# A hybrid decoder layer with a 16-expert MoE: weights loaded in groups of 128 rows, the routing of the last tile reordered, and gaps that move fp32r operands

## Chip, cores and metric

One core of a Trainium2 chip runs the whole kernel. The metric is the device time of one execution in microseconds (us). TensorE (PE) multiplies, with its weight loads shown apart as PEld; VectorE (DVE), ScalarE (ACT) and GpSimd (POOL) do the rest, and SyncE (SP) issues the weight transfers.

## What is computed

One decoder layer in fp32 on 512 tokens of width 1024: four token mixers with a gated merge, then a mixture of experts (top 1 of 4 groups, top 2 of its 4 experts), then a final RMSNorm.

```python
h = h + hybrid_mixer(rms_norm(h, norm1_g), ...)   # n @ w_in, 4 mixers, gates * (y_b @ P_b), merged @ w_out
h = h + hier_moe(rms_norm(h, norm2_g), ...)       # 16 experts, D = 1024, F = 512
return rms_norm(h, final_norm_g)

# hier_moe
in_grp = exp_logits of the best group;  top_l, top_e = lax.top_k(in_grp, 2)
hid = silu(t @ w_gate[e]) * (t @ w_up[e]) * combine[:, e]
out = sum over e of hid @ w_down[e]
```

## The kernel before

**Products.** An fp32 product is made of three fp32r matmuls: `split` (L118) cuts an operand into a high part (ACT, a copy to fp32r) and a low part (DVE, the difference), and `mm3` (L122) runs three: both high parts (L123), the streamed ("moving") operand's low part with the loaded ("stationary") operand's high part (L124), and the reverse (L125). In the groups of the trace `b<-nl,XH` names the moving operand first.

**Stages.** From the start of the span: norm and transposes to 27 us; the W_in projections with the attention between them to 286 us; gates and branch products (`b<-nh,hi` and `b<-yh,hi`) to 548 us; the output product `wo_mm` (`b<-nh,m`, `b<-woh,m`) with the routing of tiles 0 to 2 to 597 us; the routing of the last tile and the dispatch to 616 us; the experts to about 925 us; the weighted sum for the last two experts, the final norm and the stores.

**Order of the work.** PE's order is the order of the code (manual_schedule, L1043). On DVE, ACT, POOL and SP a scheduler fixes the order; each runs its list in order, and an instruction that waits holds all that stand behind it.

**Weights of the experts.** Each of the 16 experts has G (gate), U (up) and D (down), 2 MB each. `wload` (L1012) brings 1 MB at a time into a ring of 13 buffers of 1 MB, SP issuing a load as soon as a buffer is free; partition p takes rows 8p to 8p+7 of G and U (4p to 4p+3 of D), so half a weight is one 8 KB run in each partition. `gsplit` (L1215) splits 128x1024 pieces into four slots `nh`, `nl`, two ahead of their use. So the k-th row group of a product is every 8th (G, U) or 4th (D) row, and everything multiplied with it is read with a stride of 32 or 16 bytes: `h2` in `disp` (L1156), X in `xt` (L1228), H in `h_tr` (L1243) and `h_half` (L1318).

**Expert loop** (L1424 on). For expert e: half of G (L123 `b<-nh,XH`), the transposes of H of e-1 (L1247), the other half of G, the transposes of X of e+1 (L1234), D of e-1 (`x<-nh,HH`), U of e. Experts 0 and 15 have no neighbour to fill waits, so their U goes through `up_halves` (L1326): two column halves of 256, with the moving operand read in a pattern of pairs, so that the first half of H can be transposed while the second is multiplied.

**Routing.** `r_t` (L1058) transposes a tile of x, `r_mm` (L1068) makes the logits and then, on DVE, the norm's scale and the top-2 choice up to the selection matrix `Msel`; `r_h2` (L1100) makes the normed tile h2; `r_pos` (L1106) counts positions on PE (L1111, L1112), makes the one-hot `sel` of expert 0 (L1116) and then positions, scatter (POOL, L1131) and weights; `disp` (L1156) multiplies h2 by `sel` into the input of expert 0 (L1160), 8 products a tile. After the last `wo_mm` the order is r_t(3,0), half of disp(0), r_t(3,1), the other half, r_mm(3), r_pos(2), r_h2(3), disp(1), disp(2), r_pos(3), disp(3), then the counts (L1202). `ph` (L1294) are 8 one-hots made on POOL for the weights `ws`, which PE needs (L1385) between G and U of expert 0. `pT` (L1407) are 8 one-hots for the last two experts, made on POOL beside expert 14, ahead of the gather of all experts' rows (L1372).

Of the kernel before, what the change touches and what calls it, by code (L numbers as in the profile page):

```python
# [85 lines left out]
def hybrid_layer_kernel(ctx, tc, x, norm1_g, w_in, gm_norm_g, gm_ws, gm_b, conv_w, conv_b, lru_wa,  # L86
# [982 lines left out]
    def r_mm(t):  # L1069
        p = bank()  # L1070
        for k in range(KD):
            PE.matmul(p[:, :24], xTb[t % 2][:, k], wr[:, k], start=k == 0, stop=k == KD - 1)
        s2 = sm("s2", 1)
        V.tensor_tensor(s2, ss2[:, t, 0:1], ss2[:, t, 1:2], op=OP.add)
        r2 = rs2[:, t:t + 1]
        rstd(r2, s2, D)
# [20 lines left out]
        V.tensor_tensor(Msel[t], OH[:, 0], OH[:, 1], op=OP.add)  # L1097
        XS[t] = OH, ef, lg, g8, e8

    def r_h2(t):  # L1100
        h2 = h2b[t]
        V.scalar_tensor_tensor(h2, x1[:, t], rs2[:, t:t + 1], g2b, op0=OP.mult, op1=OP.mult)
        XS[t] += (h2,)

    scat = []

    def r_pos(t):
        OH, ef, lg, g8, e8, h2 = XS[t]
        p = bank()
        for tt in range(t):  # L1110
            PE.matmul(p[:, :16], ones, Msel[tt], start=tt == 0, stop=False)  # L1111
        PE.matmul(p[:, :16], upper, Msel[t], start=t == 0, stop=True)  # L1112
# [3 lines left out]
        V.tensor_scalar(sel, slot, p[:, 0:1], o0, op0=OP.is_equal, op1=OP.mult)  # L1116
# [35 lines left out]
        XS[t] = sel, h2  # L1152

    x0 = [bank("x0", 2), bank("x0", 2)]

    def disp(t, ks=range(KD)):  # L1156
        sel, h2 = XS[t]
        hv = h2.rearrange("p (q k) -> p k q", k=KD)
        for k in ks:
            PE.matmul(x0[k // 4][:, (k % 4) * 128:(k % 4 + 1) * 128], hv[:, k], sel, start=t == 0 and k % 4 == 0, stop=t == NT - 1,  # L1160
                      skip_group_check=True)

    def run(g, n=99):
# [11 lines left out]
    for t in range(NT):  # L1175
        g = wo_mm(t, 1)
        for i in range(KD):
            next(g)
            if pend:
                pend.pop(0)()  # L1180
        run(g)
        wb.append([mgp.tile([128, 2048], FT, name=f"m{t}")])
        load(len(wb))
        while pend:
            pend.pop(0)()
        no = lambda: None
        pend = [lambda t=t: r_t(t, 0), no, lambda t=t: r_t(t, 1), no, lambda t=t: (r_mm(t), r_h2(t)), no, no,
                ] + ([lambda t=t: r_pos(t - 1)] if t else [])
# [12 lines left out]
    for t in range(NT):  # L1201
        PE.matmul(pcnt[:, :16], ones, Msel[t], start=t == 0, stop=t == NT - 1)  # L1202
# [23 lines left out]
        return s  # L1226

    def xt(X, q):  # L1228
        Xv = X.rearrange("p (q k) -> p k q", k=KD)
        ps_ = []  # L1230
        for i in range(2):
            p = bank()
            for k in range(4):
                PE.transpose(p[:, k * 128:(k + 1) * 128], Xv[:, i * 4 + k], ident)  # L1234
# [7 lines left out]

    def h_tr(H):  # L1243
        p = bank()
        Hv = H.rearrange("p (q k) -> p k q", k=4)
        for k in range(4):
            PE.transpose(p[:, k * 128:(k + 1) * 128], Hv[:, k], ident)  # L1247
# [13 lines left out]
    Yt = hl_pair(hl)  # L1261
    Xt = hl_pair(hl) + hl_pair(hl2)
    Yt.append(Xt.pop())
    for X in Xt[1:]:
        G.memset(X, 0.0)
    regs = {}

    def x_load(e):
        regs[e] = G.value_load(cnt[0:1, e:e + 1], min_val=0, max_val=T)
        X = Xt[(e - 1) % 3]  # L1270
        if e == 1:
            G.dma_start(X, XE[e * CAP:e * CAP + CAP])
            return X
        for r in range(4):
# [27 lines left out]
    def run_up(k, e, js):  # L1302
# [4 lines left out]
        if js[-1] == 3 and k == "U":  # L1307
            V.tensor_tensor(H[e], H[e], pgu[k], op=OP.mult)
        elif js[-1] == 3:
            H[e] = Ht[e % 2]  # L1310
            if e in (0, NE - 1):
                o, i = [v.rearrange(a, s=2, q=128) for v, a in ((H[e], "p (s q c) -> p q s c"),
                                                                (pgu[k], "p (q s c) -> p q s c"))]
                A.activation(o, i, AF.Silu)
            else:
                A.activation(H[e], pgu[k], AF.Silu)
# [59 lines left out]
    for e in range(NE):  # L1376
# [173 lines left out]
```

## Time and profile before

| what | us |
|---|---|
| median of 3 runs | 951.55 (951.45 to 951.55) |
| the profiled execution | 951.25 |
| its span on the chip | 949.7 |
| PE busy | 922.9 |
| DVE busy | 627.8 |
| ACT busy | 538.8 |
| POOL busy | 101.2 |

The busy time of PE is a sum over overlapping matmuls: the duration of one is longer than the step from its start to the next start. A row of the timeline gives start, duration, engine, line, operation, out<-in, shape, and in brackets the idle time ahead of it and what ended it. A row of the groups gives the count, the sum of durations and the mean in ns. A row of the windows gives the busy time of PE, PEld, DVE, ACT and POOL in a stretch, then the granted PE clock as a share of full speed, the share of the DMA engines' time and GB/s.

### The profile page before, as it was taken

To read this page: it belongs to the slowest core of one execution; us is meant where nothing else is said; L and a number is where in the kernel's file an instruction comes from. 1 tells how busy PE (TensorE), PEld (TensorE's weight loads), DVE (VectorE), ACT (ScalarE), POOL (GpSimd) and SP (SyncE) were. 2 spreads that over 40 slices of the span, in tenths; PEclk is the share of its full clock that TensorE was granted. 3 is DMA by queue.
4 is the path that set the end of the run, shared out by engine and by line. 5 is a ranking of instruction groups with operands and counts; after the bars stand their busy time and mean duration, and the time that the engine had idled before them with its cause. 6 is when DMAs were issued, how large, how long until landed. Compare 5 with 4: busy or idle time off the path is not lost. (4 is left out here: it accounts for less than half of the span.)

```text
span 949.7 us, 13038 instructions
## 1 busy us (share of the span) xinstructions
PE 922.9 (97%) x4765; PEld 760.1 (80%) x4765; DVE 627.8 (66%) x1165; ACT 538.8 (57%) x837; POOL 101.2 (11%) x181
## 2 busy tenths in 40 slices
PE   8999999999999999999999999999999999999993
PEld 7979888777768888888888888977888888888882
DVE  6677457888773343444374515658989989999955
ACT  7436548558982232232263314247888888888853
POOL 2000000000000000000000011441110101110750
PEclk9999999999999999999999999999999999999997
DMA  8558456652124224222444437679999999999283
GB/s 246 143 147 283 164 192 222 218 182 89 45 74 129 65 90 131 89 89 89 133 132 163 172 117 288 253 231 332 357 355 397 377 369 382 393 386 380 66 163 110
DMA packets 90047, 195.73 MB, mean 206 GB/s; under 512 B 7388, under 2 KB 63784, under 8 KB 78712
## 3 DMA queue, kind: packets, MB, share of 16 engines
q1 hardware_dynamic: 62312, 153.56, 46.2%
q0 software_dynamic: 6528, 20.29, 7.6%
q10 hardware_dynamic: 21136, 20.98, 6.4%
q8 instruction: 39, 0.64, 0.3%
q14 instruction: 32, 0.26, 0.1%
HBM read 166.24 MB, written 34.60 MB: 211 GB/s over the span
## 5 line engine op out<-in xcount | busy, mean ns | idle before, releaser
L120 DVE TENSOR_TENSOR lo<-raw,hi 128x1024 fp32r<-128x1024 f32 (+3 forms) x70 | 79.0, 1132 | 129.4 <-ACT hi L119 129.1
L119 ACT ACTIVATE hi<-raw 128x1024 fp32r<-128x1024 f32 (+3 forms) x70 | 68.6, 986 | 161.0 <-PE b L124 88.0
L123 PE MATMUL b<-nh,XH 128*128 128x512 f32 (+1 forms) x272 | 109.9, 404 | 0.5 <-ACT XH L119 0.5
L125 PE MATMUL b<-nh,XL 128*128 128x512 f32 (+1 forms) x272 | 108.2, 398 | 0.0
L124 PE MATMUL b<-nl,XH 128*128 128x512 f32 (+1 forms) x272 | 108.1, 397 | 0.0
L123 PE MATMUL b<-nh,hi 128*128 128x512 f32 x256 | 100.1, 391 | 0.0
L124 PE MATMUL b<-nl,hi 128*128 128x512 f32 x256 | 99.8, 390 | 0.0
L125 PE MATMUL b<-nh,lo 128*128 128x512 f32 x256 | 99.7, 389 | 0.0
L123 PE MATMUL mm<-nh,hi 128*128 128x512 f32 x192 | 78.8, 410 | 1.1 <-DVE nl L235 1.1
L125 PE MATMUL mm<-nh,lo 128*128 128x512 f32 x192 | 75.2, 392 | 0.0
L124 PE MATMUL mm<-nl,hi 128*128 128x512 f32 x192 | 75.0, 391 | 0.0
L120 DVE TENSOR_TENSOR nl<-wb,nh 128x1024 fp32r<-128x1024 f32 x56 | 67.2, 1227 | 7.3 <-ACT nh L119 5.2
L120 DVE TENSOR_TENSOR nl<-m,nh 128x1024 fp32r<-128x1024 f32 x56 | 66.9, 1225 | 5.5 <-ACT nh L119 3.5
L120 DVE TENSOR_TENSOR nl<-raw,nh 128x1024 fp32r<-128x1024 f32 x52 | 62.2, 1225 | 7.6 <-ACT nh L119 6.1
L119 ACT ACTIVATE nh<-wb 128x1024 fp32r<-128x1024 f32 x56 | 58.8, 1062 | 13.5 <-PE b L125 8.2
L119 ACT ACTIVATE nh<-m 128x1024 fp32r<-128x1024 f32 x56 | 58.7, 1062 | 11.3 <-PE b L125 8.6
L119 ACT ACTIVATE nh<-raw 128x1024 fp32r<-128x1024 f32 x52 | 54.5, 1062 | 14.0 <-PE b L125 11.2
L125 PEld LDWEIGHTS b<-nh,XL 128*128 128x128 f32 x272 | 52.2, 192 | 12.0 <-DVE XL L120 0.4
L123 PEld LDWEIGHTS b<-nh,XH 128*128 128x128 f32 x272 | 52.4, 193 | 11.4 <-ACT XH L119 0.7
L124 PEld LDWEIGHTS b<-nl,XH 128*128 128x128 f32 x272 | 52.3, 192 | 10.8
L123 PEld LDWEIGHTS b<-nh,hi 128*128 128x128 f32 x256 | 48.0, 188 | 10.4 <-issue 0.2
L124 PEld LDWEIGHTS b<-nl,hi 128*128 128x128 f32 x256 | 48.1, 188 | 10.3 <-issue 0.2
(391 smaller groups left out, 2049.8 us busy)
## 6 DMA issues: line engine op xcount, KB each, us to landing
raw<-in_w_in_dram SPq DMA_DIRECT2D x30, 1024.0 KB, 5.5
XE<-MZ ACTq DMA_DIRECT2D x24, 512.0 KB, 3.8
wb<-in_moe_w_gate_dram SPq DMA_DIRECT2D x10, 1024.0 KB, 8.0
m<-in_moe_w_gate_dram SPq DMA_DIRECT2D x10, 1024.0 KB, 6.2
raw<-in_moe_w_up_dram SPq DMA_DIRECT2D x9, 1024.0 KB, 5.7
wb<-in_moe_w_down_dram SPq DMA_DIRECT2D x9, 1024.0 KB, 5.0
wb<-in_moe_w_up_dram SPq DMA_DIRECT2D x9, 1024.0 KB, 7.1
m<-in_moe_w_up_dram SPq DMA_DIRECT2D x9, 1024.0 KB, 8.3
```

The lines of the kernel that those rows point to most:

```text
L119: A.activation(hi, src, AF.Copy)
L120: return V.tensor_tensor(lo, src, hi.bitcast(FT), op=OP.subtract)
L123: PE.matmul(o, w[0], xx[0], start=first, stop=False)
L124: PE.matmul(o, w[0], xx[1], start=False, stop=False)
L125: PE.matmul(o, w[1], xx[0], start=False, stop=last)
```

## The change

**Gaps.** `slot` becomes bf16 and a 64-byte tile follows it; a 256-byte tile is put into the pool `acp` at the first gate product. Both move the addresses of what is allocated behind them. Start addresses of the fp32r operands modulo 512 bytes, as built:

| products | moving, before | stationary, before | apart | after |
|---|---|---|---|---|
| projections, gates (nh by hi) | 416 | 160 | 256 | 256 |
| branch (yh by hi) | 480 | 480 | 0 | 256 |
| wo_mm, experts (by m, X, H) | 416 | 480 | 64 | 256 |

After, the moving operands stand at 224 and the stationary ones at 480 throughout. The 512-wide products whose distance changes are 384 (branch), 192 (wo_mm) and 1104 (experts).

**Weights.** A load takes groups of 128 rows: partition p gets row p of each group, in runs of 2 KB (G, U) or 4 KB (D). All the strided reads named above become contiguous, the column halves of experts 0 and 15 among them.

**Routing.** `r_mm`, `r_pos` are cut up (norm scale `r_rs`, choice `r_top`, indices and weights `r_idx`). For the last tile the scale and h2 come ahead of the logits, disp(1) ahead of r_pos(2), and the indices of tiles 2 and 3 after `Msel` of tile 3.

**The rest.** The first load of X for experts 1 to 3 is unconditional (it was so for expert 1 alone) and two memsets on POOL go. `pT` is made on DVE.

```diff
-    slot = const([128, 128], FT, "slot")
+    slot = const([128, 128], BF, "slot")
+    V.memset(const([128, 16], FT, "gap"), 0.0)
...
+                    if not bi + dt_:
+                        V.memset(acp.tile([128, 64], FT, name="gap"), 0.0)
...
-        src = ap.rearrange("(p k) f -> p (k f)", p=128)[:, h * 2048:(h + 1) * 2048]
-        n = 2048 // len(ws)
+        n, m = 2048 // len(ws), ap.shape[0] // 256 // len(ws)
+        src = ap.rearrange("(k p) f -> p k f", p=128)
         for i, w in enumerate(ws):
-            S.dma_start(w, src[:, i * n:i * n + n])
+            k = (h * len(ws) + i) * m
+            S.dma_start(w.rearrange("p (k f) -> p k f", k=m), src[:, k:k + m])
...
-            PE.matmul(x0[k // 4][:, (k % 4) * 128:(k % 4 + 1) * 128], hv[:, k], sel, start=t == 0 and k % 4 == 0, stop=t == NT - 1,
+            PE.matmul(x0[k // 4][:, (k % 4) * 128:(k % 4 + 1) * 128], h2[:, k * 128:(k + 1) * 128], sel, start=t == 0 and k % 4 == 0, stop=t == NT - 1,
...
     r_t(3, 1)
+    r_rs(3)
+    r_h2(3)
     disp(0, range(4, KD))
-    r_mm(3)
+    r_top(3, r_mm(3))
+    disp(1)
     r_pos(2)
-    r_h2(3)
-    disp(1)
     disp(2)
     r_pos(3)
     disp(3)
+    for t in (2, 3):
+        with tc.issue_after(MS[3]):
+            r_idx(t)
...
-    for X in Xt[1:]:
-        G.memset(X, 0.0)
...
-        if e == 1:
+        if e <= len(Xt):
             G.dma_start(X, XE[e * CAP:e * CAP + CAP])
...
-                g.append([v.rearrange("p k (q s c) -> p k s q c", s=2, c=2) for v in ready.popleft()])
-            up_mm(p[s][:, :256], q[e], [v[:, :, s] for v in g[j]], j)
+                g.append(ready.popleft())
+            up_mm(p[s][:, :256], q[e], [v[:, :, s * 256:s * 256 + 256] for v in g[j]], j)
...
-                G.tensor_scalar(pT[:, t], slot, lz[:, a, 1, i:i + 1], lz[:, a, 0, i:i + 1], op0=OP.is_equal,
+                V.tensor_scalar(pT[:, t], slot, lz[:, a, 1, i:i + 1], lz[:, a, 0, i:i + 1], op0=OP.is_equal,
```

DVE before, from the logits of tile 3 (`lg`) on; `sel`, `po`, `pm`, `pcs` are tile 2's positions, `wd` and `w_` its weights:

```order
L1078 SCALAR_TENSOR_TENSOR lg<-b,rs_4852,br 128x24
L1139 TENSOR_TENSOR idx<-dd,sl 128x2
L1116 TENSOR_SCALAR sel<-slot,b,o_5388 128x128
L1080 MAX g_5365<-lg 128x8
L1118 COPY po<-b 128x16
L1082 MAX_INDEX gi_5367<-g_5365,lg 128x8
L1145 SCALAR_TENSOR_TENSOR wd<-ed,gs 128x1
L1120 TENSOR_TENSOR pm<-OH,po 128x32
L1084 CAST gi<-gi_5367 128x1
L1147 RECIPROCAL w__5419<-wd 128x1
L1122 TENSOR_REDUCE pcs<-pm 128x2
L1086 TENSOR_SCALAR pen<-g_4835,gi 128x16
```

DVE after, at the same place:

```order
L1089 MAX g_5372<-lg 128x8
L1155 TENSOR_TENSOR idx<-dd,sl 128x2
L1091 MAX_INDEX gi_5374<-g_5372,lg 128x8
L1093 CAST gi<-gi_5374 128x1
L1095 TENSOR_SCALAR pen<-g_4839,gi 128x16
L1096 TENSOR_TENSOR pen<-pen,lg 128x16
L1098 MAX e_5381<-pen 128x8
L1100 MAX_INDEX ei_5383<-e_5381,pen 128x8
L1102 CAST ef<-ei_5383 128x2
L1104 TENSOR_TENSOR OH<-e_4835,ef 128x32
L1106 TENSOR_TENSOR Msel_4854<-OH 128x16
```

Tile 2's positions and weights no longer stand among the steps from tile 3's logits to its `Msel`.

POOL before, from the norm scales of the last tiles to the first load of X; `XE` is the scatter's target (two a tile), `lo<-slot,pcs` are the one-hots `ph`:

```order
L208 TENSOR_TENSOR rs_4852<-ms,mh 128x1 x2
L1131 DMA XE<-lo,ix 3072x1024 x2
L1265 MEMSET lo 128x1024
L1131 DMA XE<-hi,ix 3072x1024 x2
L1131 DMA XE<-lo,ix 3072x1024 x2
L1265 MEMSET hi 128x1024
L1294 TENSOR_SCALAR lo<-slot,pcs 128x128 x8
L1269 TENSOR_LOAD cnt
```

POOL after:

```order
L1310 TENSOR_SCALAR lo<-slot,pcs 128x128 x2
L208 TENSOR_TENSOR rs_4856<-ms,mh 128x1
L1310 TENSOR_SCALAR lo<-slot,pcs 128x128 x2
L1147 DMA XE<-lo,ix 3072x1024 x2
L1310 TENSOR_SCALAR lo<-slot,pcs 128x128 x4
L1147 DMA XE<-hi,ix 3072x1024 x2
L1147 DMA XE<-lo,ix 3072x1024 x2
L1285 TENSOR_LOAD cnt
```

The memsets are gone, four of the one-hots stand ahead of tile 1's scatter, and all stand ahead of those of tiles 2 and 3.

DVE before, at the end of expert 14's G, where `wb`, `m` are pieces of weights and `XL`, `HL` low parts:

```order
L120 TENSOR_TENSOR HL<-b,HH 128x512
L120 TENSOR_TENSOR nl<-wb_4981,nh 128x1024
L120 TENSOR_TENSOR XL_5507<-b,XH_5506 128x512 x2
L120 TENSOR_TENSOR nl<-wb_4981,nh 128x1024
L120 TENSOR_TENSOR nl<-wb_4982,nh 128x1024 x2
```

DVE after, at the same place:

```order
L120 TENSOR_TENSOR HL<-b,HH 128x512
L120 TENSOR_TENSOR nl<-wb_4985,nh 128x1024
L1417 TENSOR_SCALAR hi<-slot,lz 128x128
L120 TENSOR_TENSOR XL_5511<-b,XH_5510 128x512 x2
L1417 TENSOR_SCALAR hi<-slot,lz 128x128 x7
L120 TENSOR_TENSOR nl<-wb_4985,nh 128x1024
L120 TENSOR_TENSOR nl<-wb_4986,nh 128x1024 x2
```

The eight one-hots `pT` stand among the low parts of the weights, seven of them in a row.

More of the change, by code (lines that the diff above doesn't have):

```diff
@@ L1054, in wo_mm @@
         sumsq(ss2[:, t, hf:hf + 1], xs, jk)
-    XS = {}
+    XS, MS = {}, {}
     def r_t(t, q):
@@ L1072, in r_mm, with r_rs, r_top @@
             PE.matmul(p[:, :24], xTb[t % 2][:, k], wr[:, k], start=k == 0, stop=k == KD - 1)
+        return p
+    def r_rs(t):
         s2 = sm("s2", 1)
         V.tensor_tensor(s2, ss2[:, t, 0:1], ss2[:, t, 1:2], op=OP.add)
+        rstd(rs2[:, t:t + 1], s2, D)
+    def r_top(t, p):
         r2 = rs2[:, t:t + 1]
-        rstd(r2, s2, D)
         lg = sm("lg", 24)
@@ L1096, in r_mm, with r_h2 @@
                         op=OP.is_equal)
-        V.tensor_tensor(Msel[t], OH[:, 0], OH[:, 1], op=OP.add)
-        XS[t] = OH, ef, lg, g8, e8
-    def r_h2(t):
+        MS[t] = V.tensor_tensor(Msel[t], OH[:, 0], OH[:, 1], op=OP.add).ins
+        o0 = sm("o0", 1)
+        V.tensor_tensor(o0, OH[:, 0, 0:1], OH[:, 1, 0:1], op=OP.add)
+        XS[t] = OH, ef, lg, g8, e8, o0
+    def r_h2(t, behind=None):
         h2 = h2b[t]
-        V.scalar_tensor_tensor(h2, x1[:, t], rs2[:, t:t + 1], g2b, op0=OP.mult, op1=OP.mult)
-        XS[t] += (h2,)
-    scat = []
+        with tc.issue_after(behind) if behind else ExitStack():
+            V.scalar_tensor_tensor(h2, x1[:, t], rs2[:, t:t + 1], g2b, op0=OP.mult, op1=OP.mult)
+        HH2[t] = h2
+    scat, HH2, SEL, PP = [], {}, {}, {}
     def r_pos(t):
-        OH, ef, lg, g8, e8, h2 = XS[t]
-        p = bank()
+        OH, ef, lg, g8, e8, o0 = XS[t]
+        p = PP[t] = bank()
         for tt in range(t):
@@ L1113, in r_pos, with r_idx @@
         sel = wop.tile([128, 128], FT, name="sel", bufs=4)
-        o0 = sm("o0", 1)
-        V.tensor_tensor(o0, OH[:, 0, 0:1], OH[:, 1, 0:1], op=OP.add)
         V.tensor_scalar(sel, slot, p[:, 0:1], o0, op0=OP.is_equal, op1=OP.mult)
+        SEL[t] = sel
+    def r_idx(t):
+        OH, ef, lg, g8, e8, o0 = XS[t]
+        p, h2 = PP[t], HH2[t]
         po = sm("po", 16)
@@ L1151, in r_pos @@
         V.tensor_copy(lz[:, t, 1], po[:, NE - 2:])
-        XS[t] = sel, h2
     x0 = [bank("x0", 2), bank("x0", 2)]
     def disp(t, ks=range(KD)):
-        sel, h2 = XS[t]
-        hv = h2.rearrange("p (q k) -> p k q", k=KD)
+        sel, h2 = SEL[t], HH2[t]
         for k in ks:
-            PE.matmul(x0[k // 4][:, (k % 4) * 128:(k % 4 + 1) * 128], hv[:, k], sel, start=t == 0 and k % 4 == 0, stop=t == NT - 1,
+            PE.matmul(x0[k // 4][:, (k % 4) * 128:(k % 4 + 1) * 128], h2[:, k * 128:(k + 1) * 128], sel, start=t == 0 and k % 4 == 0, stop=t == NT - 1,
                       skip_group_check=True)
@@ L1186, in hybrid_layer_kernel @@
         no = lambda: None
-        pend = [lambda t=t: r_t(t, 0), no, lambda t=t: r_t(t, 1), no, lambda t=t: (r_mm(t), r_h2(t)), no, no,
-                ] + ([lambda t=t: r_pos(t - 1)] if t else [])
+        pend = [lambda t=t: r_t(t, 0), no, lambda t=t: (r_t(t, 1), r_rs(t)), no,
+                lambda t=t: (r_top(t, r_mm(t)), r_h2(t, MS[t])), no, no,
+                ] + ([lambda t=t: (r_pos(t - 1), r_idx(t - 1))] if t else [])
     r_t(3, 0)
@@ L1228, in xt @@
     def xt(X, q):
-        Xv = X.rearrange("p (q k) -> p k q", k=KD)
         ps_ = []
@@ L1233, in xt @@
             for k in range(4):
-                PE.transpose(p[:, k * 128:(k + 1) * 128], Xv[:, i * 4 + k], ident)
+                c = (i * 4 + k) * 128
+                PE.transpose(p[:, k * 128:(k + 1) * 128], X[:, c:c + 128], ident)
             ps_.append(p)
@@ L1244, in h_tr @@
         p = bank()
-        Hv = H.rearrange("p (q k) -> p k q", k=4)
         for k in range(4):
-            PE.transpose(p[:, k * 128:(k + 1) * 128], Hv[:, k], ident)
+            PE.transpose(p[:, k * 128:(k + 1) * 128], H[:, k * 128:(k + 1) * 128], ident)
         HH, HL = HQ
@@ L1310, in run_up @@
             H[e] = Ht[e % 2]
[L1311 to L1316, printed above, removed]
+            A.activation(H[e], pgu[k], AF.Silu)
     def h_half(e, s):
         p = bank()
-        Hv = H[e][:, s * 256:s * 256 + 256].rearrange("p (q c) -> p c q", c=2)
         for c in range(2):
-            PE.transpose(p[:, c * 128:(c + 1) * 128], Hv[:, c], ident)
+            PE.transpose(p[:, c * 128:(c + 1) * 128], H[e][:, s * 256 + c * 128:s * 256 + c * 128 + 128], ident)
         o = [v[:, 2 * s:2 * s + 2].rearrange("p k t -> p (k t)") for v in HQ]
```

## The prediction

> **What bounds the kernel now.** I read the page's first part, then the windows by stage, then PE's groups by form, then the timeline where PE pauses.
>
> ```profile
> span 949.7 us, 13038 instructions
> PE 922.9 (97%) x4765; PEld 760.1 (80%) x4765; DVE 627.8 (66%) x1165; ACT 538.8 (57%) x837; POOL 101.2 (11%) x181
> ```
>
> ```profile
> 286.00:548.00 262.00, 262.00 (x1149) 215.47 (x1149) 114.71 (x154) 83.72 (x128) 2.87 (x6) 1.00 0.36 118
> 548.00:597.00 49.00, 49.00 (x249) 40.29 (x248) 19.92 (x79) 13.63 (x30) 8.53 (x13) 1.00 0.56 204
> 653.00:918.00 265.00, 265.00 (x1226) 217.86 (x1226) 238.78 (x231) 221.52 (x259) 55.97 (x111) 1.00 0.92 334
> ```
>
> PE fills all 262, 49 and 265 us of these stages (first figure behind the comma) at full clock (1.00). What shortens a matmul there shortens the kernel, until another engine takes over; nearest is DVE, 238.78 of 265 us busy. So the step from one matmul's start to the next is the quantity. In PE's timeline, a run of gate-like products and one of expert products:
>
> ```profile
> 161.24 0.40 PE L124 MATMUL mm<-nl,hi 128*128 128x512 f32 x1
> ...
> 165.78 0.39 PE L123 MATMUL mm<-nh,hi 128*128 128x512 f32 x1
> ```
>
> ```profile
> 894.87 0.40 PE L125 MATMUL b<-nh,XL 128*128 128x512 f32 x1
> ...
> 897.67 0.40 PE L125 MATMUL b<-nh,XL 128*128 128x512 f32 x1
> ```
>
> Twenty steps between the first pair make 4.54 us, 227 ns each; twelve between the second make 2.80 us, 233.3 ns each. Shape and clock are the same; by the table of addresses the operands stand 256 bytes apart in the first, 64 in the second. The groups say the same in durations:
>
> ```profile
> L124 PE MATMUL b<-nl,hi 128*128 128x512 f32 x256 | 99.8, 390 | 0.0
> ...
> L124 PE MATMUL b<-nl,XH 128*128 128x512 f32 x240 | 94.9, 395 | 0.0
> ...
> L123 PE MATMUL b<-yh,hi 128*128 128x512 f32 x128 | 50.4, 394 | 0.0
> L125 PE MATMUL b<-yh,lo 128*128 128x512 f32 x128 | 50.3, 393 | 0.0
> L124 PE MATMUL b<-yl,hi 128*128 128x512 f32 x128 | 49.8, 389 | 0.0
> ...
> L124 PE MATMUL b<-nl,m 128*128 128x512 f32 x32 | 12.6, 394 | 0.0
> ```
>
> At 256 bytes 390; at 64 bytes 395 in the experts, where DMA and DVE are busy, and 394 in wo_mm, where they are not; at 0 bytes 392 on the mean. Load on the other engines is thus no explanation of the difference.
>
> **The change, part by part.** *Distance.* Where 64 bytes become 256, the steps give 6.3 ns a product (233.3 less 227.0) and the durations 5 (395 less 390): I take 5.7. Where 0 becomes 256, the durations give 2 on the mean and 4 on the dearest line: I take 2.6. wo_mm: 192 x 5.7 = 1.1 us. Branch: 384 x 2.6 = 1.0. Experts: 1104 less the 48 of expert 0's G and D, which stand below, 1056 x 5.7 = 6.0. PE has no other work to wait for in these stages, so all of it is on the path. Bounds: nothing, and 6.3 ns each (1248 x 6.3 = 7.9 where I have 7.1).
>
> The Trainium skill ("SBUF — State Buffer", section "Who interferes with whom") gives PE two independent read ports, one for the moving operand and one for weight loads, and says that PE never waits on anyone; by it these 8.1 us would be zero, and the sum 8 us higher. The trace's 390 against 394 in quiet stages speaks against it.
>
> *Strided reads on the path.* Dispatch first:
>
> ```profile
> L1160 PE MATMUL x<-sel,lo 128*128 128x128 f32 x32 | 8.3, 424 | 0.5 <-DVE sel L1116 0.5
> ...
> L604 PE MATMUL mm<-w,yb 128*128 128x128 f32 x32 | 4.0, 274 | 0.0
> ```
>
> ```profile
> 603.58 4.07 PE L1160 MATMUL x<-sel,lo 128*128 128x128 f32 x16
> ...
> 607.25 0.16 DVE L1097 TENSOR_TENSOR Msel<-OH 128x16 bf16<-128x16 f32 x1
> ...
> 607.48 3.97 PE L1160 MATMUL x<-sel,hi 128*128 128x128 f32 x16
> ...
> 611.59 0.35 DVE L1116 TENSOR_SCALAR sel<-slot,b,o 128x128 f32<-128x128 f32 x1 [3.83 <-PE b L1112]
> ...
> 611.99 4.18 PE L1160 MATMUL x<-sel,lo 128*128 128x128 f32 x16 [0.45 <-DVE sel L1116]
> ...
> 616.12 0.77 PE L123 MATMUL b<-nh,XH 128*128 128x512 f32 x1
> ```
>
> A tile's 16 records take 4.0 us, 0.25 a step; contiguous ones of this size (L604, mean 274 against 424) save about 0.13 each, so a tile takes some 1.9. Msel of tile 3 is ready at 607.41, but its positions come behind disp(2), and `sel` is made at 611.59. After, disp(1) and disp(2) are over by about 606, and PE waits for Msel instead. I leave Msel at 607.4: logits come some 1.6 us earlier (half of disp(0), wo_mm), tile 2's steps no longer stand between, but h2 of tile 3 (128x1024) and `sel` of tile 2 now do. Then `sel`, tile 3's dispatch of 1.9 and the counts: G of expert 0 starts at about 610.4 instead of 616.12, 5.7 us earlier. Bounds: 4.0 (Msel 1.7 later) and 7.5 (earlier by what the logits gain).
>
> ```profile
> 622.10 1.06 PE L1385 MATMUL b<-ow,lo 128*128 128x16 f32 x8
> 624.07 0.40 PE L1385 MATMUL b<-ow,lo 128*128 128x16 f32 x2 [0.91 <-POOL lo L1294]
> ...
> 626.05 0.46 PE L123 MATMUL b<-nh,XH 128*128 128x256 f32 x1
> ```
>
> Between 622.10 and 626.05 PE makes the weights' 16 records and waits for POOL's one-hots in between: the first 8 ran freely, 0.114 a step ((1.06 less the last one's 0.26) / 7), so 16 need 1.85 of these 3.95 us, and 2.1 are waiting. After, POOL has no memset and no late scatter ahead, and all one-hots but those of tile 3 can be made before G of expert 0 begins; those have its 6 us (616.12 to 622.10) as cover. Gain 2.1. If the counts of tile 3 come 4 us later than its `sel`, the cover is used up and the gain falls to about 1; it can't be more than 2.1.
>
> *Column halves.*
>
> ```profile
> 74.29 0.28 PE L568 MATMUL mm<-hi,nl 128*128 128x256 f32 x1
> ...
> 74.77 0.28 PE L568 MATMUL mm<-lo,nh 128*128 128x256 f32 x1
> ```
>
> ```profile
> 908.34 0.41 PE L123 MATMUL b<-nh,XH 128*128 128x256 f32 x1
> ...
> 909.71 0.41 PE L123 MATMUL b<-nh,XH 128*128 128x256 f32 x1
> ```
>
> ```profile
> 626.00:644.70 18.70, 17.82 (x78) 15.03 (x78) 10.04 (x13) 8.04 (x10) 2.38 (x6) 0.91 0.78 241
> 907.60:925.40 17.80, 17.51 (x78) 14.80 (x78) 9.86 (x12) 7.43 (x10) 10.61 (x7) 1.00 1.04 197
> ```
>
> Read in pairs, a 256-wide product takes 1.37/6 = 228 ns; contiguous, 0.48/4 = 120. Each of the two experts has 48: 48 x 0.108 = 5.2 us of PE work. Not all comes through. DVE has 10 us of work in that stretch, in a chain (H, then its transposes, then HL, then products); a weight piece now feeds 12 x 0.12 = 1.44 us of PE against this much of DVE:
>
> ```profile
> L120 DVE TENSOR_TENSOR nl<-wb,nh 128x1024 fp32r<-128x1024 f32 x56 | 67.2, 1227 | 7.3 <-ACT nh L119 5.2
> ...
> L120 DVE TENSOR_TENSOR HL<-b,HH 128x512 fp32r<-128x512 f32 x14 | 9.6, 684 | 0.0
> ```
>
> 1.227 of 1.44 leaves 0.2 a piece, and the H and HL work of some 1.4 us falls behind it. I take 4.1 for expert 0 and 3.5 for expert 15 (its splits also share DVE with expert 14's result). Bounds: 2.5 and 5.2 each. Expert 0's G and D add 48 x 5.7 = 0.3. The clock: expert 0's row has 0.91, 1.7 of 18.7 us lost, yet the stretch is only 0.9 us longer than expert 15's at 1.00. So reads in pairs hide part of a slow clock, and contiguous ones would show it: I add 0.8 (bounds 0 and 1.7).
>
> *Transposes.*
>
> ```profile
> L1234 PE MATMUL b<-ident,hi 128*128 128x128 f32 x80 | 10.6, 275 | 0.0
> ...
> L1247 PE MATMUL b<-ident,H 128*128 128x128 f32 x56 | 8.8, 280 | 0.0
> ```
>
> Against 274 contiguous, 120 x 1 to 3 and 56 x 6: 0.6 us.
>
> *pT on DVE.*
>
> ```profile
> L818 DVE TENSOR_SCALAR t<-t,sm 128x128 f32<-128x128 f32 x16 | 3.9, 284 | 0.2
> ```
>
> Eight x 0.284 = 2.3 us among the low parts, at expert 14. An expert has 72 products: 72 x 0.2333 and some 1.4 for transposes are 18.2 us before, 17.8 after; DVE needs 238.78/265 of 18.2, 16.4, so 1.4 is slack and 0.9 shows. If the slack is less than that, all 2.3 show. POOL loses this work and reaches its stores and the gather of experts' rows earlier, so nothing new waits for it. Cost 0.9 (bounds 0 and 2.3). The unconditional loads of X for experts 2 and 3 and the 256 bytes of memset lie on POOL and DVE far ahead of use: nothing.
>
> *Weights by row groups.* Runs of 8 KB become 2 or 4 KB. In the DMA part the nearest prices are these:
>
> ```profile
> q10 hardware_dynamic: 21136, 20.98, 6.4%
> ```
>
> ```profile
> m<-in_moe_w_down_dram SPq DMA_DIRECT2D x9, 1024.0 KB, 8.8
> ...
> wbx<-in_w_branch_dram SPq DMA_DIRECT2D x7, 1024.0 KB, 5.0
> ```
>
> Loads in 2 KB runs land in 5.0 us (w_branch), not later than any 8 KB ones. A ring of 13 MB with 6 used per 18.2 us turns in 39 us; less landing (8.8) and splitting (3) some 27 us of lead remain. Queue 10's 1 KB packets: 6.4% of 16 x 949.7 us for 20.98 MB is 345 GB/s. The experts moved 334 GB/s on the mean (third window). At 345 GB/s an expert with 6.9 MB takes 20 us instead of 17.8 and falls behind by 2.2 each, 25 over the 11.5 experts that still load: covered by the 27. Cost 0; the bounds are 0 and the second rival's times.
>
> *Sum.* 951.25 - 1.1 (wo_mm) - 1.0 (branch) - 6.0 (experts) - 5.7 (last tile) - 2.1 (one-hots) - 4.1 - 3.5 (halves) - 0.3 - 0.6 (transposes) + 0.8 (clock) + 0.9 (pT) = 928.6, a gain of 22.7. The profiled run is 0.3 under the median of the runs, so 928.9 stands against 951.55. The end (925 on) keeps its 25 us.
>
> **Rivals.** *The distance does nothing* (the 4 to 6 ns belong to something else, or the gaps don't hold): 8.1 less, so 937 with expert 0's part. Against it: three places with one distance each and one price each. Chance 0.12.
>
> *DMA becomes the bound.* If 2 KB runs fetch markedly worse in a full queue, the lead of 27 us is used up by expert 14, and PE then waits for each load. An expert moves 6.3 MB of weights and, with its X and Y, at most 6.9 MB while the ring fills. The gain of 22.7 is eaten when 11.5 experts lose 27 + 22.7 = 50 us, 4.3 each: a DMA period of 17.8 + 4.3 = 22.1 us for 6.9 MB, 312 GB/s. Below that rate the kernel is slower than before; at 290 the period is 23.8, and the time 951.55 - 22.7 + 11.5 x 6.0 - 27 = 971, chance 0.03. A partial loss, at 325 GB/s, gives a period of 21.2 and 951.55 - 22.7 + 39 - 27 = 941, chance 0.07. For it: the packets get shorter on a queue whose engines are 0.92 busy. Against it: 345 GB/s even with 1 KB packets.
>
> The Trainium skill ("DMA: Bandwidth & Descriptors", section "Specifications") limits HBM to about 358 GB/s a core; 6.9 MB would then need 19.3 us an expert. By that limit DMA would fall behind by 1.5 us an expert, 17 in all, which the lead still covers; the trace's mean of 334 is below it, and no run here shows what 2 KB runs reach.
>
> *DVE takes it over.* If the halves come through half (2.6 each: 2.4 lost), Msel comes 1.7 late and pT costs 2.3, 1.4 more than I took: 5.5 in all, 934.4. For it: DVE's 16.4 of 17.8 us in every expert. Against it: in the two experts with halves DVE has 10 of 18 us. Chance 0.13.
>
> The forecast holds in the rest, 0.65, with 923 to 933 as its own range.
>
> **Numbers.** Predicted 928.9. All bounds of gain together (distance 7.9, branch 1.0, halves 5.2 twice, last tile 7.5, the one-hots 2.1, 0.9 of the small ones, no loss by clock or pT) make 29.8 and 921.8; with 3 us for what a timeline worked out by hand misses, the range begins at 919. It ends at 939, so that the distance without effect and DVE's case lie within. Outside lie the DMA case and tails, some 0.15. A measurement of this kernel can tell 0.2%, 1.9 us, from no change. Faster 0.95 (all but the slow end of the DMA case), same 0.01, slower 0.04 (that end, 0.03, and 0.01 for a stall that I don't see).
>
> **What would show it.** Right: groups of experts and wo_mm at 390 like the gates; L1160 near 275; G of expert 0 at 610; no POOL wait at the weights' products; 256-wide products near 285; PE without pauses from expert 1 on. Wrong: pauses of PE behind ACT or DVE that wait for loads in experts 8 to 14; groups still at 395; a new DVE wait at expert 14 of over 2 us.

## The result and the profile after

The changed kernel takes 928.41 us (median of 4 runs, 928.32 to 930.08) against 951.55: a ratio of 0.9757 (95% interval 0.974 to 0.9774), 23.1 us less. The prediction was 928.9.

The page of the changed kernel, its first lines:

```profile
span 928.3 us, 13012 instructions
PE 898.4 (97%) x4765; PEld 741.9 (80%) x4765; DVE 625.9 (67%) x1175; ACT 538.3 (58%) x837; POOL 81.6 (9%) x165
```

PE is as full as before and its busy time is 24.5 us less. Its groups by form, where line 1174 is the dispatch:

```profile
L124 PE MATMUL b<-nl,hi 128*128 128x512 f32 x256 | 99.6, 389 | 0.0
...
L124 PE MATMUL b<-nl,XH 128*128 128x512 f32 x240 | 93.7, 390 | 0.0
...
L123 PE MATMUL b<-yh,hi 128*128 128x512 f32 x128 | 49.8, 389 | 0.0
...
L124 PE MATMUL b<-nl,m 128*128 128x512 f32 x32 | 12.5, 390 | 0.0
...
L124 PE MATMUL b<-nl,XH 128*128 128x256 f32 x32 | 9.2, 286 | 0.5 <-DVE nl L120 0.5
...
L1174 PE MATMUL x<-sel,lo 128*128 128x128 f32 x32 | 4.1, 281 | 0.4 <-DVE sel L1127 0.4
```

Each 512-wide group shown now has the 389 to 390 ns that only the gates had of these; the dispatch went from 424 to 281, and the column halves to 286 from the 414 of before:

```profile
L124 PE MATMUL b<-nl,XH 128*128 128x256 f32 x32 | 13.3, 414 | 0.0
```

The last tile, all engines:

```profile
601.25 2.03 PE L1174 MATMUL x<-sel,lo 128*128 128x128 f32 x16
...
601.60 1.21 POOL L1310 TENSOR_SCALAR lo<-slot,pcs 128x128 f32<-128x128 bf16 x2 [4.42 <-PE b L1076]
602.79 0.57 POOL L208 TENSOR_TENSOR rs<-ms,mh 128x1 f32<-128x1 f32 x1
...
603.39 1.41 DVE L1114 SCALAR_TENSOR_TENSOR lo<-xm,rs,g2b 128x1024 f32<-128x1024 f32 x1 [2.53 <-POOL rs L208]
...
605.41 2.05 PE L1174 MATMUL x<-sel,hi 128*128 128x128 f32 x16 [2.08 <-DVE dd L1154]
...
607.65 0.17 DVE L1106 TENSOR_TENSOR Msel<-OH 128x16 bf16<-128x16 f32 x1
...
607.88 0.17 PE L1125 MATMUL b<-Msel,upper 128*128 128x16 bf16 x1 [0.36 <-DVE Msel L1106]
```

PE now waits for Msel (0.36 us, and 2.08 before disp(2)), as forecast. Why Msel is no earlier stands in the POOL rows: the norm scale of tile 3 (`rs`, L208) is queued behind two one-hots that had to wait until 601.60, and DVE waits 2.53 us for it. Then PE's timeline from expert 0's first product on:

```profile
611.17 0.50 PE L123 MATMUL b<-nh,XH 128*128 128x512 f32 x1 [0.54 <-ACT XH L119]
...
617.42 1.85 PE L1395 MATMUL b<-ow,lo 128*128 128x16 f32 x16
619.12 0.37 PE L123 MATMUL b<-nh,XH 128*128 128x256 f32 x1
```

The 16 records of the weights run through in 1.85 us without a wait for POOL (3.95 before). The windows of the experts:

```profile
653.00:700.00 47.00, 47.00 (x225) 39.12 (x223) 43.27 (x42) 41.65 (x49) 6.62 (x24) 1.00 1.04 380
700.00:750.00 50.00, 50.00 (x240) 41.54 (x239) 46.26 (x47) 43.51 (x53) 6.54 (x22) 1.00 1.04 368
750.00:800.00 50.00, 50.00 (x240) 41.54 (x239) 47.19 (x47) 43.21 (x51) 6.14 (x22) 1.00 1.04 378
800.00:850.00 50.00, 50.00 (x240) 41.56 (x239) 46.42 (x46) 43.68 (x52) 5.47 (x16) 1.00 1.04 381
```

PE doesn't pause, but the DMA engines are now full from end to end: their share is 1.04 (it is added up over packets and can pass 1), against 0.92 on the mean of the experts before. In the lists of DMA issues the loads of the experts' weights, which before landed after 5.0 to 8.8 us on the median, land late. One line of before, then two of after:

```profile
raw<-in_moe_w_down_dram SPq DMA_DIRECT2D x7, 1024.0 KB, 7.5
```

```profile
wb<-in_moe_w_gate_dram SPq DMA_DIRECT2D x10, 1024.0 KB, 15.1
...
raw<-in_moe_w_down_dram SPq DMA_DIRECT2D x7, 1024.0 KB, 17.3
```

Where the gain came, by the start of the same instruction in the traces. The profiled execution of the changed kernel (930.08 us, the slowest of the four) lost some 1.9 us at 280 us, where the granted clock was 0.57 on the mean of 3.5 us (279.5 to 283); the last column therefore uses the trace of the run onehots_behind_msel, whose work and order are those of the changed kernel:

| start of | before | changed | changed, second trace | gained since the row above |
|---|---|---|---|---|
| first product of wo_mm | 544.11 | 544.35 | 542.45 | 1.7 |
| last product of wo_mm | 596.78 | 596.54 | 594.61 | 0.5 |
| G of expert 0 | 616.12 | 611.17 | 609.23 | 4.7 |
| last record of the weights of expert 0 | 625.93 | 619.01 | 617.00 | 2.0 |
| D of expert 1 | 665.66 | 653.65 | 651.68 | 5.1 |
| D of expert 13 | 883.82 | 866.45 | 864.48 | 5.4 |
| D of expert 14 | 901.98 | 884.67 | 882.71 | -0.1 |
| last product of D of expert 15 | 925.14 | 903.71 | 901.74 | 4.1 |
| end of the span | 949.72 | 928.25 | 926.33 | 0.0 |

### The profile page after: what moved, and what is told of

It reads as the page before. It is cut to its first block, busy times and chain, and to the rows that moved or that the text cites. A ratio compares the mean times of both kernels' runs of the same rounds, so it can differ in the third digit from the quotient of the medians.

```text
span 928.3 us, 13012 instructions
## 1 busy us (share of the span) xinstructions
PE 898.4 (97%) x4765; PEld 741.9 (80%) x4765; DVE 625.9 (67%) x1175; ACT 538.3 (58%) x837; POOL 81.6 (9%) x165
## 5 line engine op out<-in xcount | busy, mean ns | idle before, releaser
L123 PE MATMUL b<-nh,XH 128*128 128x512 f32 (+1 forms) x272 | 104.2, 383 | 1.0 <-ACT XH L119 1.0
L125 PE MATMUL b<-nh,XL 128*128 128x512 f32 (+1 forms) x272 | 103.0, 379 | 0.3 <-DVE XL L120 0.3
L124 PE MATMUL b<-nl,XH 128*128 128x512 f32 (+1 forms) x272 | 102.8, 378 | 0.5 <-DVE nl L120 0.5
L124 PEld LDWEIGHTS b<-nl,hi 128*128 128x128 f32 x256 | 48.2, 188 | 10.4 <-issue 0.5
```

Source lines behind the costliest of these rows:

```text
L123: PE.matmul(o, w[0], xx[0], start=first, stop=False)
L124: PE.matmul(o, w[0], xx[1], start=False, stop=False)
L125: PE.matmul(o, w[1], xx[0], start=False, stop=last)
```

## The experiments

**The gaps undone.**

```diff
-    slot = const([128, 128], BF, "slot")
-    V.memset(const([128, 16], FT, "gap"), 0.0)
+    slot = const([128, 128], FT, "slot")
...
-                    if not bi + dt_:
-                        V.memset(acp.tile([128, 64], FT, name="gap"), 0.0)
```

> The changed kernel without its two gaps and with slot in fp32 again: the fp32r operands stand 256, 0 and 64 bytes apart modulo 512 as before the change, all else is kept. If the distance sets the step of a matmul, the products of wo_mm and the experts go back from about 228 to 233.5 ns a step and the branch products to 230, and the time rises by 8 to 9 us, to about 937 (ratio to the kernel before 0.985). If the distance does nothing, the time stays at 928.4 (0.976) and the steps at 228.

Measured: 937.42 us, ratio 0.9843 (0.9826 to 0.9859), 8.7 above a repeat of the changed kernel measured alongside (928.77, below). Its groups:

```profile
L124 PE MATMUL b<-nl,XH 128*128 128x512 f32 x240 | 94.8, 395 | 0.0
...
L123 PE MATMUL b<-yh,hi 128*128 128x512 f32 x128 | 50.4, 394 | 0.0
...
L124 PE MATMUL b<-nl,m 128*128 128x512 f32 x32 | 12.6, 395 | 0.0
```

The durations of before are back, with contiguous weights, the new order and full DMA engines.

**The gaps alone.**

```diff
-    slot = const([128, 128], FT, "slot")
+    slot = const([128, 128], BF, "slot")
+    V.memset(const([128, 16], FT, "gap"), 0.0)
...
+                    if not bi + dt_:
+                        V.memset(acp.tile([128, 64], FT, name="gap"), 0.0)
```

(on the kernel before)

> The kernel before with the two gaps and slot in bf16, nothing else: all fp32r operands 256 bytes apart. If the distance sets the step: 951.5 less 8 to 9 us, about 943 (ratio 0.991), with groups of the experts at 390 and steps of 228 ns. If it does nothing: 951.5. If the steps are shortened but another engine takes the gain back, the steps are 228 and PE shows pauses.

Measured: 943.19 us, ratio 0.9898 (0.9881 to 0.9914), 9.1 under the 952.27 of the kernel before measured alongside, 8.4 under its 951.55 above.

```profile
L124 PE MATMUL b<-nl,XH 128*128 128x512 f32 x240 | 93.7, 391 | 0.0
...
L123 PE MATMUL b<-yh,hi 128*128 128x512 f32 x128 | 49.8, 389 | 0.0
...
L124 PE MATMUL b<-nl,m 128*128 128x512 f32 x32 | 12.5, 391 | 0.0
```

Two gaps of 64 and 256 bytes and `slot` in bf16, which move addresses, bring 8 to 9 us with nothing else changed, and the undoing costs as much: the addresses are the cause, and no other engine takes the gain back. It isn't the address of one operand alone: by the table of addresses the gates of before had the experts' moving address (416) and 390 ns, and the experts of after have the stationary address of before (480) and 390.

**Other distances.**

```diff
+    V.memset(ep.tile([128, 32], FT, name="gap2", bufs=1), 0.0)
     HQ = [ep.tile([128, 4, 128], FR, name=f"H{n}", bufs=1) for n in "HL"]
     Ht = [ep.tile([128, FE], FT, name=f"H{i}", bufs=1) for i in range(2)]
+    V.memset(ep.tile([128, 64], FT, name="gap", bufs=1), 0.0)
```

> The changed kernel with two more gaps among the experts' tiles, so that X stands 128 bytes and H 0 bytes from the moving operand modulo 512, and all else stays 256 apart. If the cost falls steadily with the distance (0 dearest): H products at more than 233.5 ns a step, X between 228 and 233. If it is as the branch products had it (0 bytes 230.6, 64 bytes 233.5): H near 230.6, and X tells where the cost ends: 228 if it is only near 64, up to 233 if not. If the distance does nothing: 228 for both.

Measured: 932.95 us, one run. Two rows of its PE timeline 20 steps apart, and its groups:

```profile
715.04 0.39 PE L123 MATMUL b<-nh,XH 128*128 128x512 f32 x1
...
719.69 0.40 PE L125 MATMUL b<-nh,XL 128*128 128x512 f32 x1
```

```profile
L124 PE MATMUL b<-nl,XH 128*128 128x512 f32 x240 | 94.7, 395 | 0.0
...
L124 PE MATMUL x<-nl,HH 128*128 128x512 f32 x128 | 50.2, 392 | 0.2 <-DVE nl L120 0.2
```

At 128 bytes a step is 4.65/20 = 232.5 ns, nearly as dear as 64. At 0 bytes H costs what it does at 256 in the changed kernel (392). None of the three expectations holds in full: the cost doesn't fall with the distance, and 0 bytes, which cost the branch products of before 3 to 5 ns on two lines of three (394, 393, 389), cost H nothing. What sets the branch apart (its operands both began at 480 modulo 512, these at 224) was not tried.

**The halves in pairs again.**

```diff
-                g.append(ready.popleft())
-            up_mm(p[s][:, :256], q[e], [v[:, :, s * 256:s * 256 + 256] for v in g[j]], j)
+                g.append([v.rearrange("p k (q s c) -> p k s q c", s=2, c=2) for v in ready.popleft()])
+            up_mm(p[s][:, :256], q[e], [v[:, :, s] for v in g[j]], j)
```

> The changed kernel with the column halves of U of experts 0 and 15 read in pairs again (their columns are then mixed up, so these two experts are computed wrongly; work and counts are the same). PE work rises by 96 x 0.108 = 10.4 us. If the halves came through as the prediction took it: 4.1 + 3.5 on the path less the 0.8 of clock, so about 7 us slower, 935.3. If DVE holds PE up by half: 5.2 slower, 933.6. If all comes through: 938.8.

Measured: 937.9 us, ratio 0.9844 (0.9826 to 0.9861): 9.5 above the changed kernel. By the landmarks of its trace the loss is 4.6 at expert 0 and 4.0 at expert 15, 8.6 of the 10.4 us of PE work. So DVE holds PE up for less than I took. The group of the halves is back at the duration of before:

```profile
L124 PE MATMUL b<-nl,XH 128*128 128x256 f32 x32 | 13.2, 411 | 0.0
```

The granted clock of this trace is 0.51 from 621.0 to 624.4, in U of expert 0, where the kernel before had its slow stretch too. From the first of the 48 paired products to the last it is 11.05 us there and 10.98 at expert 15, at full clock: the slow stretch cost the paired products next to nothing.

**The dispatch strided again.**

```diff
-            PE.matmul(x0[k // 4][:, (k % 4) * 128:(k % 4 + 1) * 128], h2[:, k * 128:(k + 1) * 128], sel, start=t == 0 and k % 4 == 0, stop=t == NT - 1,
+            PE.matmul(x0[k // 4][:, (k % 4) * 128:(k % 4 + 1) * 128], h2.rearrange("p (q k) -> p k q", k=KD)[:, k], sel, start=t == 0 and k % 4 == 0, stop=t == NT - 1,
```

> The changed kernel with h2 read with a stride of 32 bytes in the dispatch again (the channels of expert 0's input are then mixed up, so expert 0 is computed wrongly). PE work rises by 64 x 0.13 = 8.2 us. If the dispatch of tiles 1 and 2 lies beside DVE's chain to Msel of tile 3, as the prediction has it, part is hidden: disp(0) 2 and disp(3) 2 show, and of disp(1) and disp(2) what exceeds the 2.4 us that PE waits there, 1.7: 5.7 slower, 934.1. If PE's order alone counts: 8.2 slower, 936.6.

Measured: 934.43 us, ratio 0.9809 (0.9791 to 0.9826), 6.0 above the changed kernel (5.3 by the landmarks of the trace). Of 8.2 us of PE work 2 to 3 don't show, as worked out. But its granted clock is 0.50 from 604.7 to 608.1 and from 611.6 to 618.4, in the last tile, where the changed kernel's is 1.00; how much of the 5.3 us the slower clock has wasn't separated, so the agreement with 5.7 may be partly luck. The weight loads show the price of the stride, here and then in the changed kernel:

```profile
L1174 PEld LDWEIGHTS x<-sel,hi 128*128 128x128 f32 x32 | 7.8, 333 | 0.6 <-DVE sel L1127 0.6
```

```profile
L1174 PEld LDWEIGHTS x<-sel,hi 128*128 128x128 f32 x32 | 3.8, 192 | 2.2 <-DVE dd L1154 2.2
```

**The last tile in the order of before.**

```diff
     r_t(3, 1)
-    r_rs(3)
-    r_h2(3)
     disp(0, range(4, KD))
-    r_top(3, r_mm(3))
-    disp(1)
+    p3 = r_mm(3)
+    r_rs(3)
+    r_top(3, p3)
     r_pos(2)
+    r_idx(2)
+    r_h2(3)
+    disp(1)
     disp(2)
     r_pos(3)
+    r_idx(3)
     disp(3)
-    for t in (2, 3):
-        with tc.issue_after(MS[3]):
-            r_idx(t)
```

> The changed kernel with the last tile's order of before: scale, logits, choice, then positions, indices and h2 as before, disp(1) behind r_pos(2). The dispatch is contiguous. If the shorter dispatch brought the gain: within 1 us of 928.4. If the order did: the choice of tile 3 comes behind tile 2's steps again, and positions and one-hots late, so G of expert 0 starts 2 to 4 us later and the wait for the one-hots at the weights of expert 0 (2.1) is back: 931 to 934.

Measured: 929.3 us, ratio 0.9765 (0.975 to 0.978). Counted from the last product of wo_mm, as in the changed kernel's second trace, G of expert 0 starts 0.65 us earlier, the weights are ready 0.25 later (part of PE's wait for the one-hots is back), and 0.2 is left at the end. The medians differ by 0.9 us and the intervals overlap. So the reordering as built brought nothing that these runs can tell; the shorter dispatch brought the gain. The logits wait for the norm scale (`rs`) on POOL in this order too:

```profile
602.36 0.24 DVE L1087 SCALAR_TENSOR_TENSOR lg<-b,rs,br 128x24 f32<-128x24 f32 x1 [1.99 <-POOL rs L208]
```

**The one-hots behind Msel.**

```diff
     for i in range(2 * NT):
-        G.tensor_scalar(ph[:, i], slot, pcs[:, i // 2, i % 2:i % 2 + 1], None, op0=OP.is_equal)
+        with tc.issue_after(MS[3]):
+            G.tensor_scalar(ph[:, i], slot, pcs[:, i // 2, i % 2:i % 2 + 1], None, op0=OP.is_equal)
```

> The changed kernel with the one-hots of the weights (ph) issued on POOL only after Msel of tile 3. In the changed kernel the norm scale of tile 3 stands on POOL behind two of these one-hots, which wait until 601.6 for a buffer; DVE waits 2.5 us for it. If that wait is on the path to Msel of tile 3 and so to expert 0: G of expert 0 starts about 2 us earlier (609 instead of 611.2), and the time falls by 1.5 to 2.2 us unless the one-hots then come too late for the weights of expert 0, which would give back up to 2. If the path is DVE's own list and not the wait: no change, 928.4.

Measured: 928.77 us, ratio 0.9752 (0.9736 to 0.9768). The edit did nothing: Msel is made on DVE, and in the trace POOL runs the same list in the same order as in the changed kernel. So nothing is learned of the wait here; the run is a repeat of the changed kernel and shows how closely one is measured again: 0.4 us.

**The norm scale first on POOL.**

```diff
-        rstd(rs2[:, t:t + 1], s2, D)
+        MS["rs"] = rstd(rs2[:, t:t + 1], s2, D)
...
     for i in range(2 * NT):
-        G.tensor_scalar(ph[:, i], slot, pcs[:, i // 2, i % 2:i % 2 + 1], None, op0=OP.is_equal)
+        with tc.issue_after(MS["rs"]):
+            G.tensor_scalar(ph[:, i], slot, pcs[:, i // 2, i % 2:i % 2 + 1], None, op0=OP.is_equal)
```

(`rstd` returns its POOL instruction)

> The changed kernel with the norm scale of tile 3 ahead of the first one-hots (ph) in POOL's list; the edit before, onehots_behind_msel, left that list as it was. If DVE's 2.5 us wait for the scale is on the path: logits and Msel of tile 3 come 2.2 us earlier, G of expert 0 starts 1.5 to 2.2 us earlier against the landmark before it (the last logits product to G: 10.0 us now, 8 then), and the time is 926.3 to 927. If DVE's own list or PE's disp(1) and disp(2) end as late anyway: 928.4.

Measured: 927.55 us, ratio 0.9742 (0.9723 to 0.9761), by time alone not to be told from the changed kernel. Its timeline:

```profile
598.78 0.57 POOL L208 TENSOR_TENSOR rs<-ms,mh 128x1 f32<-128x1 f32 x1 [3.43 <-DVE ms L202]
...
603.71 0.17 DVE L1106 TENSOR_TENSOR Msel<-OH 128x16 bf16<-128x16 f32 x1
...
607.52 0.50 PE L123 MATMUL b<-nh,XH 128*128 128x512 f32 x1 [0.66 <-ACT XH L119]
```

Against the second trace of the changed kernel G starts 1.7 us earlier: the wait was on the path. At the end 0.9 is left, since PE then waits for the X of expert 1, a load that stands on POOL behind the scatters. PE's timeline of this run:

```profile
630.49 1.09 PE L1253 MATMUL b<-ident,hi 128*128 128x128 f32 x8 [0.82 <-DMA hi<-XE]
```

**pT on POOL again.**

```diff
-                V.tensor_scalar(pT[:, t], slot, lz[:, a, 1, i:i + 1], lz[:, a, 0, i:i + 1], op0=OP.is_equal,
+                G.tensor_scalar(pT[:, t], slot, lz[:, a, 1, i:i + 1], lz[:, a, 0, i:i + 1], op0=OP.is_equal,
```

> The changed kernel with the eight one-hots of the last two experts on POOL again. If they cost PE about 0.5 us on DVE and are hidden on POOL: 928.0, 0.4 faster, without the delay of expert 14 against expert 13. If POOL's 15 us of work delay the gather past the end of expert 15, which now comes earlier: slower by 2 to 8 us, with a wait for the gather in the final sum.

Measured: 928.57 us, ratio 0.9749 (0.9732 to 0.9766), not to be told from the changed kernel by time. In the trace the step from D of expert 13 to D of 14 is 17.74 us (18.23 with pT on DVE), so DVE's version costs 0.5, and nothing ends later.

**Both mends together.** The two edits above in one kernel.

> The changed kernel with both small mends: the norm scale of tile 3 first in POOL's list (measured alone at 0.9 us by the landmarks of its trace) and the one-hots of the last two experts on POOL (0.5). If both add up: 1.4 us less, 927.0, ratio to the kernel before 0.974. If the later gather now ends the kernel, only 0.9 less.

Measured: 927.11 us, ratio 0.9741 (0.9728 to 0.9754), the fastest median of all and 1.3 us under the changed kernel; the intervals overlap. Its trace ends 0.75 us earlier than the changed kernel's second one, because the X of expert 1 is later still:

```profile
631.10 1.09 PE L1253 MATMUL b<-ident,hi 128*128 128x128 f32 x8 [1.58 <-DMA hi<-XE]
```

**Runs of 1 KB.**

```diff
-            S.dma_start(w.rearrange("p (k f) -> p k f", k=m), src[:, k:k + m])
+            wv = w.rearrange("p (k f) -> p k f", k=m)
+            for c in range(0, ap.shape[1], 256):
+                S.dma_start(wv[:, :, c:c + 256], src[:, k:k + m, c:c + 256])
```

> The changed kernel with every expert weight loaded in column blocks of 256, so in runs of 1 KB (two or four transfers in place of one). It asks how near the DMA rival is. If 1 KB runs move 345 GB/s as queue 10's do: 20.0 us an expert against 17.7, 26 us behind over the last 11.5 experts against a lead of 28: no more than 1 us slower, with the landing time of loads at over 20 us by expert 12. If they move 309 GB/s: 22.3 us an expert, 53 less 28, so 25 us slower, 953, with PE pausing in the last six experts.

Measured: 957.46 us, ratio 1.0061 (1.0041 to 1.0081), 29 above the changed kernel and slower than the kernel before. Windows of its experts:

```profile
700.00:750.00 50.00, 50.00 (x240) 41.54 (x239) 46.26 (x46) 44.12 (x52) 6.66 (x24) 1.00 1.08 329
750.00:800.00 50.00, 50.00 (x240) 41.54 (x239) 46.84 (x47) 42.92 (x52) 6.08 (x20) 1.00 1.09 340
800.00:850.00 50.00, 45.32 (x209) 36.05 (x208) 40.09 (x39) 35.77 (x43) 5.50 (x16) 1.00 1.09 344
```

DMA moves 329 to 344 GB/s where the changed kernel's runs of 2 KB (G, U) and 4 KB (D) moved 368 to 381. For 150 us PE doesn't notice; then the lead is used up, and PE has 45.32 of 50. Most of the loss comes at the end: from D of expert 14 to D of expert 15 it is 32.6 us instead of 13.2. There loads that are now late (the last are issued at 914.7) overlap the gather of the experts' rows, which begins at 888.5; in the changed kernel the last load was issued at 862.6 and the gather began at 878.7. A window of that stretch, and ACT's row there:

```profile
900.00:905.00 5.00, 0.00 (x0) 0.00 (x0) 0.00 (x0) 0.00 (x0) 3.00 (x2) 0.75 1.07 226
```

```profile
908.81 1.06 ACT L119 ACTIVATE nh<-raw 128x1024 fp32r<-128x1024 f32 x1 [12.82 <-DMA raw<-in_moe_w_up_dram]
```

With the gather among them the full DMA engines move 226 GB/s (at 885 to 890, the changed kernel's gather, they move 200). PE waits 10.55 us in one piece, and its granted clock is then 0.55 on the mean from 900 to 926, so not all of these 19.4 us is DMA alone. Neither expectation held: the rate is near the first, the loss beyond the second.

**As many transfers, in runs of 2 KB.**

```diff
-            S.dma_start(w.rearrange("p (k f) -> p k f", k=m), src[:, k:k + m])
+            wv = w.rearrange("p (k f) -> p k f", k=m)
+            for i in range(0, m, max(m // 2, 1)):
+                for c in range(0, ap.shape[1], 512):
+                    j = slice(i, i + max(m // 2, 1))
+                    S.dma_start(wv[:, j, c:c + 512], src[:, k + j.start:k + j.stop, c:c + 512])
```

> The changed kernel with as many transfers as runs_of_1k, but in runs of 2 KB (rows cut by groups, D's also in two column halves). If the number of transfers (SP's issues) made runs_of_1k slow: about as slow, 950 to 957. If the length of the runs did: near 928.4, at most 932, with loads landing some us later.

Measured: 928.64 us, ratio 0.9758 (0.9743 to 0.9773), the changed kernel's time. Window of its experts:

```profile
750.00:800.00 50.00, 50.00 (x240) 41.55 (x239) 47.12 (x47) 43.41 (x51) 6.06 (x20) 1.00 1.05 371
```

So at these sizes the length of the runs decides, not the number of transfers.

## Why the prediction was right

**Distance.** Taken as 8.1 and 0.3 us, measured as 8.7 (undone) and 8.4 to 9.1 (alone). The branch was under-sized: 1.0 taken, 1.7 gained up to wo_mm. By the mean steps of the traces 1.3 of this are the branch and 0.4 the gates, whose distance didn't change (227.2 to 226.7 ns); why those gained stays open. wo_mm's stage shows 0.5 of its 1.1. From first product to last it takes 52.7 us before and 51.7 with the gaps alone, 53.1 with the gaps undone and 52.2 changed: the distance gives the 0.9 to 1.0 it was to give, and the rest of the change, which reorders the routing of tiles 0 to 2 in that stage too, costs 0.4 to 0.5. The prediction has no term for that. Experts 2 to 13 gain 0.45 us each, 5.4 together; the terms of the sum for them were 0.41 and some 0.04 for transposes. The rival without effect of the distance is out: the rule of the Trainium skill ("SBUF — State Buffer", section "Who interferes with whom") that PE's two read ports are independent and that PE waits for no one doesn't describe these products, since the same matmul takes 390 or 395 ns by the addresses of its two operands.

**Last tile.** Taken 5.7, measured 4.7. That PE would wait for Msel instead of the dispatch was right. Leaving Msel where it was came close: counted from the last product of wo_mm its step starts after 10.5 us before (607.25 less 596.78) and 11.1 after (607.65 less 596.54). That the clock time agrees (607.4) is luck, since 607.65 holds the 1.9 us that this execution lost at 280 us; in the second trace it is 605.7. The cause was incomplete: I counted DVE's h2 and `sel` and didn't follow the norm scale into POOL's list, where it stands behind one-hots that wait for a buffer. Without that wait G starts 1.7 us earlier (scale_first). The forecast for G isn't clear either: 610.4 already has wo_mm's gain among its reasons, and the sum subtracts wo_mm and the branch once more. Altogether G came 6.9 us earlier, between the 5.7 of that landmark and the 7.8 of the sum.

**One-hots.** Taken 2.1, measured 2.0 for the stretch with G. The old order gives back 0.9 of it; what the rest comes from (the memsets, the scatters on POOL) wasn't tried apart.

**Halves.** Taken 4.1 and 3.5 less 0.8 for the clock; undoing them costs 4.6 and 4.0. DVE's hold-up was over-sized by half a microsecond each. The 0.8 for the clock had no ground: the slow stretch didn't come (the granted clock from 616 to 653 us is 1.00), and the kernel before had lost next to nothing by it (11.01 us for the 48 paired products of expert 0, 10.97 for those of expert 15). What contiguous halves lose at half the clock no run shows. A loss by the clock came elsewhere in the profiled run, at 280 us, and isn't in the second trace of this program.

**pT.** Taken 0.9, measured 0.5. The size of the work was right (2.3 taken; 0.34 and 1.88 us in DVE's rows of the trace), so some 1.7 us were covered where the mean slack said 1.4.

**DMA.** Cost 0 was right for 2 KB runs, but the lead shrank: loads that landed after 5 to 9 us land after 8 to 17. The limit of about 358 GB/s a core that the prediction takes from the Trainium skill ("DMA: Bandwidth & Descriptors", section "Specifications") didn't show: the experts' windows move 368 to 381, and slices of the profile of before up to 397. The bound was too kind: 345 GB/s at 1 KB was to be covered by the lead, and the kernel with 1 KB runs, at 329 to 344 GB/s, is 29 us slower than the changed one. I had counted only the lead, and not that late loads meet the gather at the end. The rival's mechanism is real, and one halving of the run length of G and U away.

The errors (last tile 1.0 and wo_mm 0.6 too much; halves with the clock 1.8, the stretch up to wo_mm 0.7 and pT 0.4 too little) partly cancel; with 23.1 measured against 22.7 the sum is better than its terms, and that is luck.

## What to carry to other kernels

Compare the mean of the same matmul shape between stages before looking for stalls: 5 ns in 390, in a stage where PE never pauses, was 8 to 9 us here and went away with two unused tiles of 64 and 256 bytes and one constant in bf16. When an engine's list changes, follow what it hands to the others: the tail lost 1.7 us to a one-element-wide instruction on POOL behind work that waited for a buffer, in the new order of the steps, and in the old one it waited too. And when PE gets faster beside a full DMA, look at the landing times, not only at PE's pauses: the lead shrinks long before anything stops.

## What the runs showed of the hardware

The cost by the operands' distance modulo 512 bytes isn't a slope. The means of the steps of the X products in the traces are 227.6 ns at 256 bytes, 232.5 at 128 and 233.3 at 64; at 0 bytes H costs nothing more and the branch products 3 ns. What decides at 0 stays open. A moving operand read in pairs of fp32 (8 of every 16 bytes) takes 228 ns for 256 columns against 120 contiguous, as long as 512 contiguous ones (227). The Trainium skill ("SBUF — State Buffer", section "Door 1: The DMA port swizzle") says that two hits in a 16-byte line keep full bandwidth; these pairs have two, and the trace shows half the rate. A stationary fp32 operand read with a stride of 32 bytes loads in 333 ns against 192.

The granted clock went with these reads. All three traces in which U of expert 0 is read in pairs (before, gaps alone, halves in pairs) have some 3.4 us at half clock in it (0.51 to 0.53); none of the eleven with contiguous halves has. All three traces with a strided dispatch have one or two such stretches between 600 and 619 us (means of 0.91, 0.82 and 0.73); the eleven with a contiguous one have 1.00. It is one trace of each kernel, and the cause isn't shown.
